# First layer: four conv chunks of w_in ahead of v, built up by quarters of the modulation

## The chip, the cores and the metric

The kernel runs on one core of one Trainium2 chip. The metric is the device time of one execution in microseconds (us). Engines are TensorE (PE, its weight loads PEld), VectorE (DVE), ScalarE (ACT), GpSimd (POOL) and SyncE (SP), which here issues nearly all DMA transfers.

## What is computed

A two-layer block over 512 tokens of x and 256 tokens of a context, 1024 features wide. For each layer:

```
mx, mc = split(silu(c) @ w_ada + b_ada, 6), the same of c_ctx      # the modulation
hx = rmsnorm(x, g) * (1 + mx[1]) + mx[0]; hc likewise with mc
z  = [hx; hc] @ w_in          # columns: q, k, v, o (512 each), 16 gates, fourier 256, conv a 256, conv t 256
u  = a * sigmoid(t);  yv = silu(layernorm(dwconv(u, 31 taps) + b_dw))
ym = mLSTM over q, k, v and the gates (4 heads, forward and backward), normed, times sigmoid(o)
yf = real part of a 2-D FFT of the fourier columns
x += mx[2] * rmsnorm(concat(ym, yf, yv) @ w_out);  x += mx[5] * rmsnorm(mlp(modulated norm of x))
```

The context takes the same steps in the first layer.

## The kernel before, in words

Tokens are in six blocks of 128: blocks 0 and 1 are the context, 2 to 5 are x. Features are in KB = 8 blocks of 128. The modulated, normalised input lies transposed in `hhi` and `hlo` (128 partitions, 8 feature blocks, 768 tokens): every fp32 operand is split into a high part and a rest, and each product is three matmuls, hi x hi, hi x lo, lo x hi. A weight is loaded by SP into one of three `raw` slots (L214), then ScalarE writes hi (L220) and VectorE writes lo = raw - hi (L221); there are six slots for hi and five for lo. `weight(...)` takes the next weight of the list `stream` and prepares up to `ahead` more.

Instructions are written in program order. A planner then orders each engine's instructions when the program is built: it prefers earlier ones but passes over what it reckons isn't ready. At run time each engine and each queue follows its order. `tc.cur_priority + LATER` (300) puts the conv taps behind 300 later instructions in that preference.

*Start of layer 0.* The modulation needed first (shift and scale of the mixers) comes in four quarters of its columns (`ada_first`). A quarter is 2 MB of w_ada, loaded by L299 into whatever slots are free (`rooms`: raw, hi, lo, t4 or halves of t3 tiles), multiplied with silu(c) (L313), given its bias (L316), turned into columns (L319, L320), scaled (L381) and applied by `prenorm_k` to two feature blocks of transposed x (transposes L446, then L453 on ScalarE, L233 and L234 on VectorE). The order of feature blocks is `KORD` = 0, 4, 1, 5, 2, 6, 3, 7, two per quarter. Between the quarters TensorE multiplies what is modulated with the first half of the v columns (`v_mm`, L511: 128 tokens stationary, 264 columns moving, 256 of v and 8 of gates), for the four x blocks in four `mm` PSUM banks. Then the context is loaded (L563), normalised (`unit`: L409, L398, L403, L411), modulated, and v is finished: 2 column halves x 6 blocks x 24 matmuls = 288. `v_out` evicts each (L516 on ScalarE, L517 on VectorE).

*After v.* The 16 gate columns in `gs` are transposed (L613) and pass through exp, ln and three-part scans on VectorE (L614 to L640), a round trip through DRAM (`md`, L638 to L653), and `gate_columns` (L659 to L671). Meanwhile `CHUNKS` runs: conv t0, a0, t1, a1, then q, k, o of four heads, then fourier. Each chunk is 128 columns of w_in by `stationary` (L464: 24 pairs of matmuls, 256 context tokens and 512 tokens of x, in two mm banks). t chunks end in a tanh (L967), a chunks in u = (tanh + 1) * a (L974). After a1 come `gate_columns` and the 62 taps of the depthwise convolution on VectorE (L688, L690), seven per chunk. Head h (`mlstm`) starts after chunk o of that head. After each chunk `background` runs three steps of the other modulations (a 512 KB load of w_a, L246, into a raw slot, and L248 on TensorE); they fill the same three raw slots as the weights.

Of the kernel before, what the change touches and what calls it, by code (L numbers as in the profile page):

```python
# [65 lines left out]
def build(tc, a):  # L66
# [216 lines left out]
    def ada_first(res):  # L283
# [4 lines left out]
        lo_ = lambda: lop.tile([128, 1024], F32, tag="lo", name=nm("raw"))  # L288
# [186 lines left out]
    def layer(l, res, nbg, first=None):  # L475
# [22 lines left out]
        vt = [t3()[:, :NB * 129].rearrange("p (b n) -> p b n", b=NB) for _ in range(H)]  # L498
        for h in range(H):
            P.memset(vt[h][:, :, 128:129], 1.0)  # L500
        gs = t3()[:, :NB * 128].rearrange("p (b n) -> p b n", b=NB)
        P.memset(gs, 0.0)
        gv = gs.rearrange("p b (g d n) -> p b g d n", g=2, d=2)
# [15 lines left out]
        if first is None:  # L519

# [24 lines left out]
        else:  # L545
            steps, xn = first[:2]
            xb = list(range(CB, NB))
            ps, ws = {}, ([], [])
# [6 lines left out]
            def some(c, bs, ms, p):  # L555
                for b in bs:
                    if (c, b) not in ps:
                        ps[c, b] = p()
                    v_mm(ps[c, b], b, ms, ws[c])

            ct = [t4() for _ in range(CB)]
            for b in range(CB):
                dma(ct[b], a["ctx"][128 * b:128 * b + 128, :])  # L563
# [3 lines left out]
            ws[0].append(weight("v", l, 0, 0, ahead=0))  # L567
            normed(0, pt)
            for q in range(4):
                if q == 3:  # L570
                    some(0, xb, [6, 7], mm)
                    break
                pt = [turned(xn, KORD[2 * q + 2 + m], 0) for m in range(2)]
                some(0, xb, [2 * q], mm)
                next(steps)
                if q < 2:
                    ws[0].append(weight("v", l, 0, q + 1, ahead=0))
                some(0, xb, [2 * q + 1], mm)
                next(steps)
                normed(q + 1, pt)  # L580
            ws[1][:] = [weight("v", l, 1, i, ahead=0) for i in range(2)]
            for b in xb:
                v_out(ps[0, b], 0, b)
            for b in range(CB):
                xn[b] = unit(ct[b])
# [3 lines left out]
            some(1, xb, range(2), mm)  # L589
            pt = [turned(xn, KORD[m], 1) for m in range(2)]  # L590
            for m in range(KB):
                if 2 <= m < VKB[1][1]:
                    some(1, xb, [m], mm)
                prenorm_k(pt.pop(0), KORD[m], res["Amix"], res["ac", 0], 0, 1)
                if m + 2 < KB:
                    pt.append(turned(xn, KORD[m + 2], 1))
            some(0, range(CB), range(KB), aux)
            for b in range(CB):
                v_out(ps[0, b], 0, b)
            ws[1].append(weight("v", l, 1, 2))  # L600
            some(1, xb, range(VKB[2][0], KB), mm)
            for b in xb:
                v_out(ps[1, b], 1, b)
            some(1, range(CB), range(KB), mm)
            for b in range(CB):
                v_out(ps[1, b], 1, b)
# [65 lines left out]

        y = {}


        u, cacc, tg = {}, {}, {}

        def conv_taps():
            for j in range(2):
                cacc[j] = t3()  # L680
            o0 = 0 if not last else XU
            o1 = UW - 2 * PAD
            for k in range(31):
                for j in range(2):
                    o = cacc[j][:, o0:o1]
                    w = hcol(C_DW, 2 * k + j)
                    if k == 0:
                        V.tensor_scalar(o, u[j][:, o0:o1], w, cols[:, C_BDW + j:C_BDW + j + 1], ALU.mult, ALU.add)  # L688
                    else:
                        V.scalar_tensor_tensor(o, u[j][:, o0 + k:o1 + k], w, o, ALU.mult, ALU.add)  # L690
                    yield

        def ccol(b):
            return 128 * b if b < CB else XU + 128 * (b - CB)

        def conv_norm():
            yt = [t3(), t3()]
            y[6], y[7] = yt
            for g in ([[2, 3, 4, 5]] if last else [[0, 1], [2, 3, 4, 5]]):
                xns, pss = [], []  # L700
                ba = tiny.tile([128, 4, 2], F32, tag="ba", name=nm("ba"))
                for i, b in enumerate(g):
                    if i % 2 == 0:
                        pss.append(aux())
                    for j in range(2):
                        c0 = 256 * (i % 2) + 128 * j
                        T.transpose(pss[-1][:, c0:c0 + 128], cacc[j][:, ccol(b):ccol(b) + 128], ident)
                for i in range(len(g)):
                    moments(pss[i // 2][:, 256 * (i % 2):256 * (i % 2) + 256], ba[:, i])
                r = rsd(ba, len(g))  # L710
                for i in range(len(g)):
                    if i % 2 == 0:
                        xns.append(c2())
                    cb = slice(256 * (i % 2), 256 * (i % 2) + 256)
                    V.tensor_scalar(xns[-1][:, cb], pss[i // 2][:, cb], ba[:, i, 0:1], r[:, i:i + 1],
                                    ALU.subtract, ALU.mult)
                yield
                back = [aux(), aux()]
                for i in range(len(g)):
                    for j in range(2):  # L720
                        c0 = 256 * (i % 2) + 128 * j
                        T.transpose(back[j][:, 128 * i:128 * i + 128], xns[i // 2][:, c0:c0 + 128], ident)
                n = 128 * len(g)
                t0 = 128 * g[0]
                for j in range(2):
                    z = yt[j][:, t0:t0 + n]
# [170 lines left out]
        def fourier(ws):  # L897
# [32 lines left out]
            for (t0, n) in segs:  # L930
                m = n // 2
                for pr in range(2):
# [6 lines left out]
                    V.tensor_tensor(yt[:, 1:m], yt[:, 1:m], ps[:, m + 1:n], ALU.add)  # L939


        taps = None
        got = {}
        staged = []

# [5 lines left out]
        for i, (n, j) in enumerate(CHUNKS):  # L951
# [16 lines left out]
            elif n == "a":  # L968
# [6 lines left out]
                if j == 1:  # L975
                    taps = conv_taps()
                    gate_columns()
# [499 lines left out]
```

## Time and profile before

| | us |
|---|---|
| three runs | 1513.02, 1516.81, 1517.34 (median 1516.81) |
| profiled execution, its own time | 1513.57 |
| its span, first to last instruction | 1511.9 |
| TensorE busy | 1471.7 (97%) |
| VectorE busy | 1093.8 (72%) |
| ScalarE busy | 757.9 (50%) |

The granted TensorE clock is 0.999 of full speed over the span. The time around the span is 1513.57 - 1511.9 = 1.67 us. Times in views count from the span's start.

### The profile page before, as it was taken

Reading aid. Unit: us, or ns where it says so; the run is one execution under the profiler, and the core shown is the slowest. Engines: PE = TensorE matmul, PEld = TensorE weight load, DVE = VectorE, ACT = ScalarE, POOL = GpSimd, SP = SyncE. Lnnn points to the kernel's source line nnn. Section 1 sums busy time; section 2 is a strip of 40 time slices with the busy share of each in tenths; the row PEclk is TensorE's granted clock in tenths of the full one; section 3 lists DMA queues with packets and bytes.
Section 4 is the critical chain, followed back from the end, with each engine's and each line's share of the span. In section 5 each row is a group of like instructions: output and inputs, shape, how many; then the busy total and the mean of one; then the engine's idle time right before and its main releaser. Section 6 shows DMA issues by size and latency. Waiting matters only on the chain. (4 is left out here: it accounts for less than half of the span.)

```text
span 1511.9 us, 23296 instructions
## 1 busy us (share of the span) xinstructions
PE 1471.7 (97%) x8894; PEld 1292.6 (85%) x8894; DVE 1093.8 (72%) x2155; ACT 757.9 (50%) x1523; POOL 84.4 (6%) x233
## 2 busy tenths in 40 slices
PE   7899999999999999999999999999999999999997
PEld 4878888987888898898988978888888889998887
DVE  3449987854899886766866576799666977667666
ACT  4632345535745352442524576544557555555544
POOL 0000012200000000000000010011111000000000
PEclk9999999999999999999999999999999999999999
DMA  8645436523532452432622252422225142333234
GB/s 317 156 140 206 158 122 219 207 70 123 183 126 96 144 193 72 166 136 88 195 76 92 80 183 97 133 84 76 107 84 180 43 126 98 112 112 100 83 95 143
DMA packets 68128, 197.32 MB, mean 131 GB/s; under 512 B 14064, under 2 KB 16528, under 8 KB 68016
## 3 DMA queue, kind: packets, MB, share of 16 engines
q1 hardware_dynamic: 66576, 191.11, 37.7%
q0 software_dynamic: 1440, 4.72, 1.0%
q8 instruction: 70, 1.15, 0.3%
q14 instruction: 42, 0.34, 0.1%
HBM read 183.14 MB, written 12.66 MB: 130 GB/s over the span
## 5 line engine op out<-in xcount | busy, mean ns | idle before, releaser
L220 ACT ACTIVATE hi<-raw 128x1024 fp32r<-128x1024 f32 (+1 forms) x245 | 244.0, 1000 | 375.8 <-PE mm L1074 141.6
L1074 PE MATMUL mm<-hi,t 128*128 128x512 f32 (+1 forms) x1296 | 406.4, 392 | 0.1
L221 DVE TENSOR_TENSOR lo<-raw,hi 128x1024 fp32r<-128x1024 f32 (+1 forms) x245 | 280.2, 1146 | 62.7 <-ACT hi L220 28.7
L1074 PEld LDWEIGHTS mm<-hi,t 128*128 128x128 f32 x1296 | 242.3, 188 | 54.9 <-DVE t L234 1.1
L1074 PE MATMUL mm<-lo,t 128*128 128x512 f32 (+1 forms) x648 | 253.4, 391 | 0.0
L464 PE MATMUL mm<-hhi,hi 128*128 128x256 f32 (+1 forms) x576 | 167.9, 336 | 0.0
L464 PE MATMUL mm<-hlo,hi 128*128 128x256 f32 (+1 forms) x576 | 165.8, 332 | 0.0
L464 PE MATMUL mm<-hhi,lo 128*128 128x256 f32 (+1 forms) x576 | 165.2, 331 | 0.0
L1074 PEld LDWEIGHTS mm<-lo,t 128*128 128x128 f32 x648 | 121.9, 188 | 26.3
L1143 PE MATMUL mm<-hhi,hi 128*128 128x384 f32 (+1 forms) x448 | 138.5, 309 | 1.8 <-ACT c L1169 1.7
L1143 PE MATMUL mm<-hhi,lo 128*128 128x384 f32 (+1 forms) x448 | 138.1, 308 | 1.5 <-DVE lo L221 1.5
L1242 DVE TENSOR_TENSOR t<-mm,t 128x512 f32<-128x512 f32 x120 | 81.6, 687 | 78.6 <-PE mm L1074 78.6
L1143 PE MATMUL mm<-hlo,hi 128*128 128x384 f32 (+1 forms) x448 | 138.0, 308 | 0.0
L464 PEld LDWEIGHTS mm<-hhi,hi 128*128 128x128 f32 x576 | 106.7, 188 | 14.9 <-issue 2.9
L464 PEld LDWEIGHTS mm<-hhi,lo 128*128 128x128 f32 x576 | 108.2, 188 | 10.8
L464 PEld LDWEIGHTS mm<-hlo,hi 128*128 128x128 f32 x576 | 107.8, 188 | 11.3 <-issue 0.8
L690 DVE SCALAR_TENSOR_TENSOR t<-t,half,t 128x783 f32<-128x783 f32 (+1 forms) x120 | 101.8, 886 | 0.4
L1143 PE MATMUL mm<-t,hi 128*128 128x384 f32 (+1 forms) x448 | 97.2, 308 | 0.0
L1143 PEld LDWEIGHTS mm<-hhi,hi 128*128 128x128 f32 x448 | 84.2, 188 | 3.9 <-ACT c L1169 2.2
L1143 PEld LDWEIGHTS mm<-hhi,lo 128*128 128x128 f32 x448 | 84.2, 188 | 1.9 <-DVE lo L221 1.9
L234 DVE TENSOR_TENSOR t<-c,t 128x256 fp32r<-128x256 f32 (+1 forms) x132 | 62.1, 477 | 32.5 <-ACT t L231 31.7
L1143 PEld LDWEIGHTS mm<-hlo,hi 128*128 128x128 f32 x448 | 84.2, 188 | 1.2
(254 smaller groups left out, 2706.1 us busy)
## 6 DMA issues: line engine op xcount, KB each, us to landing
raw<-w SPq DMA_DIRECT2D x128, 512.0 KB, 4.1
raw<-w_at SPq DMA_DIRECT2D x48, 512.0 KB, 3.5
raw<-w_a SPq DMA_DIRECT2D x44, 512.0 KB, 4.6
raw<-w_c SPq DMA_DIRECT2D x32, 512.0 KB, 4.2
xd<-t SPq DMA_DIRECT2D x20, 512.0 KB, 3.9
raw<-w_o SPq DMA_DIRECT2D x16, 512.0 KB, 5.3
t<-xd SPq DMA_DIRECT2D x20, 256.0 KB, 6.5
t<-x SPq DMA_DIRECT2D x8, 512.0 KB, 7.8
```

Source lines behind the costliest of these rows:

```text
L220: S.activation(hi[:, r0:n0], raw[:, r0:n0], AF.Copy)
L221: V.tensor_tensor(lo[:, r0:n0], raw[:, r0:n0], hi[:, r0:n0].bitcast(F32), ALU.subtract)
L234: V.tensor_tensor(blk_lo, src, blk_hi.bitcast(F32), ALU.subtract)
L464: T.matmul(o[:, :n], wp[:, k, :], hp[:, k, t0:t0 + n], start=k == 0 and i == 0, stop=k == KB - 1 and i == 2)
L690: V.scalar_tensor_tensor(o, u[j][:, o0 + k:o1 + k], w, o, ALU.mult, ALU.add)
L1074: T.matmul(ps, hp[:, 128 * b:128 * b + 128], wp[:, f % 2, c0:c1], start=f == fs[0] and at[0] == 0 and n == 0, stop=f == fs[-1] and at[1] = ...
L1143: T.matmul(ps[:, :HN], wp[:, K2 * j + k, :], hp, start=first and k == 0 and i == 0, stop=k == K2 - 1 and i == 2, skip_group_check=True)
L1242: V.tensor_tensor(ac_, ps, ac_, ALU.add)
```

## The change

In layer 0 the four conv chunks come first, and v after them. The weights' list is reordered to match. `ada_first` loads the chunks' weights in place of the first half of w_v: two chunks behind quarter 0, two behind quarter 1, and the context behind quarter 2; the quarters lie in other slots (quarter 0 in four hi slots, quarter 1 in eight halves of t3, quarter 2 in two hi slots and four halves, quarter 3 in eight halves). Transfers of w_ada by halves of t3 are 256 KB, the others 512 KB.

The chunks are built up in the quarters for the 512 tokens of x, in four mm banks: quarter 0 with chunks 0 and 1, quarter 1 with chunks 2 and 3 too. The context is normalised after quarter 0 and modulated quarter by quarter. Its 256 tokens are multiplied apart from x: chunks 0 and 1 in two aux banks, chunks 2 and 3 in mm banks when x is done. Then v runs densely over six blocks and two halves; after each block two conv taps are written, after each third block a `background`. Then come the gates as before, q0, k0, with `gate_columns` after k0 (in layer 1 it stays after a1), o0 and the rest, with seven taps per chunk until the 62 are done.

```diff
     for l in range(DEPTH):
+        if l == 0:
+            for i, (n, j) in enumerate(CHUNKS[:4]):
+                stream.append(((n, l, j), a["w_c"][l, i], (KB, 128)))
...
         for i, (n, j) in enumerate(CHUNKS):
+            if l == 0 and i < 4:
+                continue
...
-        rooms = ((raw_, raw_, raw_, t4), (hi_, hi_, hi_, lo_), (lo_, raw_, raw_, raw_), (half_,) * 6 + (raw_,))
+        rooms = ((hi_,) * 4, (half_,) * 8, (hi_,) * 2 + (half_,) * 4, (half_,) * 8)
...
-            if q < 3:
-                pre["v", 0, 0, q] = t3()[:, :264 * (VKB[q][1] - VKB[q][0])]
-                dma(pre["v", 0, 0, q].rearrange("p (k n) -> p k n", n=264), a["w_v"][0, 0, :, VKB[q][0]:VKB[q][1], :])
+            if q < 2:
+                for i in (2 * q, 2 * q + 1):
+                    key = (CHUNKS[i][0], 0, CHUNKS[i][1])
+                    pre[key] = raw_()
+                    dma(pre[key].rearrange("p (k n) -> p k n", k=KB), a["w_c"][0, i])
+            elif q == 2:
+                res["ct"] = [t4() for _ in range(CB)]
+                for b in range(CB):
+                    dma(res["ct"][b], a["ctx"][128 * b:128 * b + 128, :])
...
+        def tap(n):
+            for _ in range(n):
+                if conv["taps"] is None:
+                    return
+                prio = tc.cur_priority
+                tc.cur_priority = prio + LATER
+                done = next(conv["taps"], 1) == 1
+                tc.cur_priority = prio + 1
+                if done:
+                    staged.append(conv_norm())
+                    conv["taps"] = None
...
+            def normed_ctx(q):
+                for k in KORD[2 * q:2 * q + 2]:
+                    prenorm_k(turned(xn, k, 1), k, res["Amix"], res["ac", 0], 0, 1)
+            def take(i):
+                cw.append(weight(CHUNKS[i][0], l, CHUNKS[i][1], ahead=0))
+            def some(items, v, p):
+                t0, n = CX[v]
+                for j, m in items:
+                    if (j, v) not in ps:
+                        ps[j, v] = p()
+                    (hi, lo), k = cw[j], KORD[m]
+                    for i, (wp, hp) in enumerate(((hi, hhi), (hi, hlo), (lo, hhi))):
+                        T.matmul(ps[j, v][:, :n], wp[:, k, :], hp[:, k, t0:t0 + n],
+                                 start=m == 0 and i == 0, stop=m == KB - 1 and i == 2)
+            def done(v):
+                for j in range(4):
+                    conv_in(*CHUNKS[j], ps[j, v], *CX[v])
+            next(steps)
+            pt = [turned(xn, KORD[m], 0) for m in range(2)]
+            next(steps)
+            take(0)
+            take(1)
+            normed(0, pt)
+            for b in range(CB):
+                xn[b] = unit(res["ct"][b])
+            plan = (([(0, 0), (1, 0)], [(0, 1), (1, 1)]),
+                    ([(j, m) for j in (2, 3) for m in (0, 1)], [(j, m) for m in (2, 3) for j in range(4)]),
+                    ([(j, 4) for j in range(4)], [(j, 5) for j in range(4)]))
+            for q in range(3):
+                pt = [turned(xn, KORD[2 * q + 2 + m], 0) for m in range(2)]
+                if q == 1:
+                    take(2)
+                    take(3)
+                some(plan[q][0], 1, mm)
+                next(steps)
+                some(plan[q][1], 1, mm)
+                next(steps)
+                normed(q + 1, pt)
+                normed_ctx(q)
+            some([(j, m) for j in range(2) for m in range(6)], 0, aux)
+            some([(j, m) for m in (6, 7) for j in range(4)], 1, mm)
+            normed_ctx(3)
+            done(1)
+            some([(j, m) for j in range(2) for m in (6, 7)], 0, aux)
+            some([(j, m) for j in (2, 3) for m in range(KB)], 0, mm)
+            done(0)
...
+            vt, gs, gv = v_tiles()
+            conv["taps"] = conv_taps()
+            for c in range(2):
+                ws = [weight("v", l, c, i) for i in range(len(VKB))]
+                for b in range(NB):
+                    ps_ = mm()
+                    v_mm(ps_, b, range(KB), ws)
+                    v_out(ps_, c, b)
+                    tap(2)
+                    if b % 3 == 2:
+                        background()
...
         for i, (n, j) in enumerate(CHUNKS):
+            if first is not None and i < 4:
+                continue
...
             elif n == "k":
                 got["k"] = short_conv(outs, lambda k: dk[:, k, j:j + 1], ranges)
+                if first is not None and j == 0:
+                    gate_columns()
```

`conv_in` holds the tanh and the product that the chunk loop held (L967 to L974), for one range of tokens; `v_tiles` allocates what stood ahead of v (L497 to L503).

## Rows read from the trace of the kernel before

**Rows 1.** Page, part 1: busy us (share of the span) and instructions.

```profile
PE 1471.7 (97%) x8894; PEld 1292.6 (85%) x8894; DVE 1093.8 (72%) x2155; ACT 757.9 (50%) x1523; POOL 84.4 (6%) x233
```

**Rows 2.** Stretches: length, PE, PEld, DVE, ACT, POOL busy (instructions), clock, DMA share, GB/s.

```profile
26.00:48.70 22.70, 20.07 (x271) 16.95 (x271) 9.94 (x26) 6.50 (x11) 0.00 (x0) 1.00 0.83 238
48.70:60.00 11.30, 9.70 (x76) 9.24 (x77) 4.64 (x11) 9.87 (x26) 1.43 (x8) 1.00 0.65 132
60.00:79.20 19.20, 19.20 (x158) 19.20 (x157) 7.83 (x19) 10.07 (x27) 0.00 (x0) 1.00 0.35 111
79.20:95.00 15.80, 15.80 (x109) 13.02 (x109) 9.57 (x10) 8.83 (x13) 0.00 (x0) 1.00 0.29 102
95.00:111.00 16.00, 13.92 (x93) 10.63 (x91) 7.07 (x9) 1.27 (x2) 0.00 (x0) 1.00 0.70 211
111.00:160.00 49.00, 49.00 (x339) 39.82 (x339) 45.97 (x64) 14.60 (x31) 2.91 (x20) 1.00 0.52 184
```

**Rows 3.** Waits of TensorE, 22.5 to 60 us: us in total, times, longest.

```profile
PE mm L511 <- DVE hhi L233: 1.8, 1, 1.8
PE mm L511 <- DVE t L517: 0.9, 1, 0.9
PE aux L313 <- ACT c L453: 0.8, 2, 0.4
PE aux L446 <- ACT t L411: 0.7, 1, 0.7
```

**Rows 4.** Waits of TensorE, 60 to 111 us.

```profile
PE aux L248 <- DMA raw<-w_a: 2.1, 2, 1.4
```

**Rows 5.** Waits of TensorE, 111 to 320 us.

```profile
PE aux L785 <- DVE c L889: 3.2, 3, 1.2
```

**Rows 6.** Stretches again, PE and PEld of L511 alone, then of L464 alone.

```profile
60.00:79.20 19.20, 19.20 (x152) 18.70 (x150) 1.00 0.35 111
...
80.30:88.40 8.10, 8.04 (x46) 7.02 (x46) 1.00 0.14 55
```

**Rows 7.** Timeline of ScalarE, 19 to 62 us: start, us, instruction, [idle before].

```profile
24.96 1.61 ACT L220 ACTIVATE hi<-t 128x792 fp32r<-128x792 f32 x2
...
32.47 1.44 ACT L453 ACTIVATE c<-aux,ac,A 128x512 f32<-128x512 f32 x2 [5.89 <-PE aux L446]
```

**Rows 8.** Timeline of VectorE, 0 to 125 us.

```profile
26.57 0.98 DVE L221 TENSOR_TENSOR lo<-t,hi 128x792 fp32r<-128x792 f32 x1
...
82.30 0.95 DVE L618 SCALAR_TENSOR_TENSOR t<-t 64x768 f32<-64x768 f32 x1 [2.20 <-ACT t L615]
...
95.89 0.95 DVE L640 TENSOR_TENSOR t<-t,t 64x768 f32<-64x768 f32 x1
96.87 1.23 DVE L221 TENSOR_TENSOR lo<-raw,hi 128x1024 fp32r<-128x1024 f32 x1
```

**Rows 9.** Transfers from 0 to 44 us, GB/s in 40 slices of 1.1 us.

```profile
GB/s 0 68 113 359 380 305 197 357 405 386 402 417 417 402 409 395 414 417 417 409 400 413 417 413 417 385 385 394 404 378 102 19 15 4 156 417 406 416 408 355
```

**Rows 10.** Timeline of SP's DMA queue, 10 to 62 us: start, us of issuing.

```profile
23.08 6.56 SPq L299 DMA_DIRECT2D t<-w_a  x6
36.41 0.33 SPq L299 DMA_DIRECT2D raw<-w_a  x1
...
46.22 7.08 SPq L354 DMA_DIRECT2D bac<-bcol  x2
53.40 0.95 SPq L214 DMA_DIRECT2D raw<-w_c  x2
```

**Rows 11.** Stretches, L690 (conv taps) alone: length, DVE busy (instructions), clock, DMA.

```profile
111.00:165.00 54.00, 33.48 (x34) 1.00 0.49 170
```

**Rows 12.** Waits of SP's queue, 0 to 125 us: us in total, times, longest.

```profile
SPq L246 <- DVE lo L221: 8.0, 3, 6.2
...
SPq L299 <- DMA raw<-w_a: 7.0, 8, 1.1
SPq L299 <- PE aux L313: 6.9, 3, 5.9
```

More of the change, by code (lines that the diff above doesn't have):

```diff
@@ L495, in layer, with conv_in @@
             yield "norm", res["Amix"]
[L498 to L503, printed above, removed]
+        y, u, cacc, tg = {}, {}, {}, {}
+        staged = []
+        conv = {"taps": None}
+        def conv_in(n, j, o, t0, m):
+            if n == "t":
+                if j not in tg:
+                    tg[j] = t3()
+                S.activation(tg[j][:, t0:t0 + m], o[:, :m], AF.Tanh, scale=0.5)
+                return
+            if j not in u:
+                u[j] = t3()
+                for z0 in (0, PAD + CTX, UW - PAD):
+                    P.memset(u[j][:, z0:z0 + PAD], 0.0)
+            d0 = PAD if t0 == 0 else 2 * PAD + CTX
+            V.scalar_tensor_tensor(u[j][:, d0:d0 + m], tg[j][:, t0:t0 + m], 1.0, o[:, :m], ALU.add, ALU.mult)
@@ new lines, in tap, with conv_taps @@
+        def tap(n):
+            for _ in range(n):
+                if conv["taps"] is None:
+                    return
+                prio = tc.cur_priority
[5 more added lines that the diff above has]
+                    conv["taps"] = None
+        def conv_taps():
+            for j in range(2):
+                cacc[j] = t3()
+            o0 = 0 if not last else XU
+            o1 = UW - 2 * PAD
+            for k in range(31):
+                for j in range(2):
+                    o = cacc[j][:, o0:o1]
+                    w = hcol(C_DW, 2 * k + j)
+                    if k == 0:
+                        V.tensor_scalar(o, u[j][:, o0:o1], w, cols[:, C_BDW + j:C_BDW + j + 1], ALU.mult, ALU.add)
+                    else:
+                        V.scalar_tensor_tensor(o, u[j][:, o0 + k:o1 + k], w, o, ALU.mult, ALU.add)
+                    yield
@@ L588, in layer @@
             dma(bd, a["bd"])
[L589 to L606, printed above, removed]
+            vt, gs, gv = v_tiles()
+            conv["taps"] = conv_taps()
[8 more added lines that the diff above has]
+                        background()
         li, x = t3()[0:64, :TOK], t3()[0:64, :TOK]
@@ L671, in gate_columns @@
             S.activation(dec, dec, AF.Exp)
[L673 to L726, printed above, removed]
-                    th = c2()
-                    S.activation(z, back[j][:, :n], AF.Identity, scale=hcol(C_GLN, j), bias=hcol(C_BLN, j))
-                    S.activation(th[:, :n], back[j][:, :n], AF.Tanh, scale=hcol(C_GLN, j), bias=hcol(C_BLN, j))
-                    V.scalar_tensor_tensor(z, th[:, :n], 1.0, z, ALU.add, ALU.mult)
-                yield
@@ L986, in layer @@
                 staged.append(mlstm(j, got["q"], got["k"], to))
-            if taps is not None:
-                for _ in range(TAPS):
-                    prio = tc.cur_priority
-                    tc.cur_priority = prio + LATER
-                    done = next(taps, 1) == 1
-                    tc.cur_priority = prio + 1
-                    if done:
-                        staged.append(conv_norm())
-                        taps = None
-                        break
+            tap(TAPS)
             background()
-        if taps is not None:
-            for _ in taps:
+        if conv["taps"] is not None:
+            for _ in conv["taps"]:
                 pass
```

89 lines of the change are left out of this document (50 added, 39 removed).

## Prediction

> **What bounds the kernel now.** I read the engine shares first: TensorE is busy for 97% of the span [rows 1], so a reordering without new arithmetic can win only what TensorE stands still, and lose only where it makes it stand. The table of stretches then says where that is [rows 2]. From 26.0 to 48.7 us, where the four quarters of the first modulation arrive, TensorE is busy 20.07 of 22.70 us (2.63 lost); from 48.7 to 60.0 it is busy 9.70 of 11.30 (1.60 lost); then it is full until 95.0, loses 2.08 us until 111.0, and is full again until 160. The waits name the losses. Between 22.5 and 60 us [rows 3]: 1.8 us for hhi of the last quarter (nothing is left to multiply until it is modulated), 0.9 us for a PSUM bank that v's eviction L517 frees, 0.8 us where the next quarter's L313 waits until L453 frees an aux bank, 0.7 us for the normalised context (L411). Between 60 and 111 us all 2.1 us are L248 waiting for its w_a block [rows 4]. After 111 us, 3.2 us are head outputs, three times, for VectorE [rows 5]. So about 4.2 + 2.1 + 3.4 = 9.7 us can be had at the very most; what it idles before 22.5 us belongs to x and quarter 0, whose transfers stay in front.
>
> VectorE matters for the second half of the change: it is busy 7.83 of 19.2, 9.57 of 15.8 and 7.07 of 16.0 us in the stretches from 60 to 111 us, then 45.97 of 49.0 [rows 2].
>
> **The change, part by part.** *Matmuls.* Layer 0 keeps its 288 matmuls of v and the 192 of the four conv chunks. In the dense v stretch 152 L511 run in 19.20 us, 0.126 us each at most; 46 L464, pairs of 256 and 512 columns, take 8.10 us, 0.352 a pair [rows 6]. Now the 512s and the 256s run apart. The 264-column v matmuls show that narrow ones keep their pace alone; 256/264 of 0.126 is 0.122, which leaves 0.230 for a 512. I take 0; the bounds are plus or minus 96 x 0.004 = 0.4 us.
>
> *The quarters.* Before, a quarter feeds TensorE 24 matmuls of v, 24 x 0.126 = 3.0 us. After, quarter 0 gives 12 x 0.230 = 2.8 us, quarter 1 gives 36 x 0.230 = 8.3, quarter 2 gives 24 x 0.230 = 5.5, and 36 context matmuls, 36 x 0.122 = 4.4 us, stand ready before quarter 3 is needed. These 4.4 us cover the 1.8 us wait; it goes, and comes back whole if the context is late. The 0.9 us bank wait goes too: the mm banks are now freed by conv_in while 12 context matmuls (1.5 us) run; without that cover it stays 0.9. The 0.7 us goes, because the context is normalised from quarter 0 on. The 0.8 us I keep: two context transposes more per quarter use the same four aux banks; bounds 0 and 2.4 (all three quarters waiting as long as both waits of the row together). Gain 1.8 + 0.9 + 0.7 = 3.4 us.
>
> *Splits.* The first weights are 1024 columns, not 792. Before, ScalarE makes the two hi parts from 24.96 in 1.61 us [rows 7] and VectorE the first lo by 26.57 + 0.98 = 27.55 [rows 8]. Scaled by columns, c0's hi comes 0.2 us later and c1's lo, the last that quarter 0 needs, at about 29. The eight hi-only matmuls (1.8 us) and quarter 1's L313 lie in front of it. I charge 0.5 us, bounds 0 and 1.5.
>
> *Transfers.* SP's order changes. Ahead of quarter 2 come 4 x 512 KB of w_c in place of 396 + 396 KB of w_v: 1.26 MB more, 3.1 us at 410 GB/s [rows 9]. Summing the slices of that row, quarter 2's last byte (9.8 MB) is in by about 28 us; 31 us is still ahead of its use, which follows the L453 of 32.47 [rows 7], at about 33.3. Ahead of quarter 3's end come 2.0 MB more (w_c and context, less w_v), 5.0 us. But in the kernel before its last block waits at 36.41, because its raw slot is held until quarter 2's L313 has read it (a wait of 5.9 us [rows 12]): transfers pause about 5 us (the slices of 102 to 156) [rows 9, 10]. Quarter 3 now lies in t3 tiles, so the pause goes and the bytes take its place: 0, hidden by quarter 1's 8.3 us of matmuls. The change moves 20 blocks of 256 KB where there were 6. The six of before went out at 23.08 to 29.64 [rows 10], and the slices there hold 378 to 417 GB/s [rows 9], so I charge nothing. The Trainium skill (DMA: Bandwidth & Descriptors, Measured) speaks against this: it wants transfers of 1 MiB or more, and lists 341 GB/s at 1 MB and 138 at 64 KB; by the 341 the 9.4 MB of w_c, context and three quarters would take, as an estimate, 4.7 us longer than at 410; the slices of the trace differ from it.
>
> The new wait is the fourth w_c block. There are three raw slots, so it can leave only when c0's lo is written, about 26.57 + 1.23 = 27.8 us [rows 8]. Its turn in SP's order comes earlier: L299 waits eight times for a transfer before it [rows 12], so some eight blocks are under way, and the turn is there when about 6.4 MB have landed, 20 us [rows 9]. Behind it: quarter 2, context, quarter 3. I take 0, since the order on SP is not the program's: layer 1's bias (L354) leaves at 46.22, ahead of the w_c blocks of 53.40 [rows 10], so what isn't ready is passed. The other bound is a rival.
>
> *Conv taps.* 34 of them take 33.48 us after 111 us [rows 11]; 24, some 24 us, are now put into v's 288 x 0.126 = 36 us, where VectorE otherwise has v's small copies and six splits of about 1 us: hidden. If they delay a copy that frees a bank, three other mm banks of 3.0 us each cover it. VectorE is freed of them later. Of the 3.2 us of L785 waits I take 0.6, half of the longest; bounds 0 and 3.2.
>
> *Gates and background.* L613 to L640 move from beside the conv chunks to beside q0 and k0. Before, the scans hold VectorE until 95.89 + 0.95, and the split of a w_c block starts right behind at 96.87 [rows 8]; SP's w_a loads wait 8.0 us in all for such splits [rows 12], and that is how L248 comes to stand 2.1 us. During v there are no scans, only taps: I take back 1.0, and leave the rest, because the scans now meet the splits of k0 and o0. Bounds 2.1 back, or 2.1 more.
>
> Sum: -3.4 + 0.5 - 0.6 - 1.0 = -4.5 us. The profiled execution took 1513.57 us (span 1511.9), so 1509.1; the median of the runs is 1516.81, and in proportion 1512.3.
>
> **Rivals.** *More goes.* If all rows of waits from 26 us on fall, 9.7 us: 1507. For it: TensorE's slack may be larger than its idle time. Its weight loads are busy 16.95 of 22.70 us in the quarters, 75%, against 18.70 of 19.20, 97%, in the dense stretch [rows 2, 6]; against it, many loads there belong to short 32-column L313. The Trainium skill (Perfetto Trace Analysis, Identifying the Most-Contended Engine) says that matmul busy time is a poor measure of headroom and weight-load share a good one; by it, at 97%, the quarters lose 22.70 - 16.95/0.97 = 5.2 us instead of 2.63.
>
> *The waits only move.* Context transposes and four splits crowd the aux banks and ScalarE; each quarter's chain gets as much longer as its cover. 3.4 us stay, the time is 1516. For it: TensorE's order is fixed, and a wait at its head holds all behind it.
>
> *SP stands at the fourth block: slower.* If that load is ordered ahead of quarter 2, nothing leaves from 20 to 27.8 us. What is under way (8.5 MB in all) has landed by 25; quarter 2 then ends at 27.8 + 1.5 + 2.6/0.41 = 35.7 us (1.5 from the load of 36.41, whose bytes show in the slices from 37.4 on), 2.4 late against its use at 33.3. The context is in at 38.3, with L409 and L411 behind it (1.1 to 1.2 us each, twice), so that its transposes can hold TensorE up to 7 us more: -4.5 + 9.4 = +4.9, 1521.7. It decides when fewer than three of quarter 2's loads pass the fourth block.
>
> *Gates late.* The chain from L618 (82.30) to L640's end (96.84) is 14.5 us [rows 8], plus the md round trip, where VectorE is 94% busy [rows 2]. Before, most of three conv chunks, 24 x 0.352 = 8.4 us each, lie between it and L659; after, q0 and k0 alone, 16.9 us, and L659 stands in TensorE's order behind them. Taken as 3 us of waiting there, and at L248 2.1 more in place of 1.0 less: 1518.
>
> *Half-size blocks slow the transfers*, the rule above: at the 378 of the lowest full slice in place of 410 [rows 9], 9.4 MB take 2.0 us longer, mostly covered: 1513. I give it 0.03 inside the second rival.
>
> **Numbers.** Forecast 0.44 (its own range 1509 to 1516), more goes 0.18, waits only move 0.18, SP stands 0.12, gates late 0.08. What a measurement of this kernel can tell from no change is about 0.3%, 4.5 us. The forecast lies on that edge, so half of it counts as faster: 0.22 + 0.18 = 0.40. Same: the other 0.22, 0.14 of the moved waits, 0.04 of the gates = 0.40. Slower: 0.12 + 0.04 + 0.04 = 0.20. The range, from the larger gain to the standing queue, is 1506 to 1521.
>
> **What would show it.** Right: no wait for hhi of the last quarter; no wait of L299 for L313 on SP; the last quarter's L453 later than 47 us without TensorE idling; first taps before 90 us; fewer than 2 us lost between 26 and 60. Wrong: TensorE waiting at a context transpose or at L313 for w_a; an SP wait of several us before quarter 2's loads; a wait at L659; VectorE's splits late during q0 and k0. The prediction fails most easily through the order that the planner gives TensorE, which the trace of before can't show.

## The result, and the profile after

The changed kernel takes 1525.67 us (median of 4, 1523.45 to 1527.33) where the kernel before, timed beside it, takes 1515.65 (1513.02 to 1517.34): a ratio of 1.0067, 95% interval 1.0045 to 1.0088. It is slower, and the time lies above the predicted range. The profiled execution has a span of 1523.0 us, 11.1 more than before. The page's first part answers to [rows 1]: hardly any work was added.

```profile
PE 1476.5 (97%) x8894; PEld 1293.9 (85%) x8894; DVE 1095.5 (72%) x2155; ACT 758.6 (50%) x1523; POOL 86.6 (6%) x233
```

The same stretches as in [rows 2], and two short ones within them:

```profile
22.50:26.00 3.50, 2.84 (x72) 2.08 (x69) 2.43 (x7) 1.45 (x2) 0.00 (x0) 1.00 1.05 410
26.00:48.70 22.70, 18.41 (x136) 14.21 (x129) 8.43 (x15) 12.05 (x18) 2.26 (x13) 0.85 0.79 243
48.70:60.00 11.30, 9.25 (x100) 7.13 (x100) 4.76 (x13) 4.81 (x8) 0.53 (x8) 1.00 0.65 133
60.00:79.20 19.20, 18.27 (x124) 16.27 (x123) 8.79 (x19) 7.85 (x16) 0.00 (x0) 1.00 0.20 60
79.20:95.00 15.80, 15.80 (x141) 14.90 (x140) 15.76 (x22) 2.65 (x9) 0.00 (x0) 1.00 0.51 186
95.00:111.00 16.00, 15.91 (x141) 14.57 (x143) 14.61 (x20) 4.45 (x12) 0.00 (x0) 1.00 0.49 163
111.00:160.00 49.00, 45.27 (x326) 36.19 (x319) 46.13 (x66) 19.02 (x41) 1.81 (x1) 0.97 0.53 166
...
28.70:35.10 6.40, 5.77 (x13) 4.35 (x14) 5.12 (x7) 3.89 (x5) 0.00 (x0) 0.50 0.58 194
147.90:151.40 3.50, 3.50 (x16) 2.13 (x15) 3.50 (x8) 1.37 (x4) 0.00 (x0) 0.53 0.45 71
```

The column to look at is the clock, which was 1.00 in every row of [rows 2]. From 28.7 to 35.1 us it is 0.50, the lower of the two levels (1.2 of 2.4 GHz). There 13 products take 5.80 us (29.33 to 35.13), and 13 of the same take 3.05 us from 37.03 on: 2.75 us lost while TensorE counts as busy. At 147.9 to 151.4 us it is 0.53, which costs 1.6 us more (0.47 of 3.5).

Length minus PE busy, against before, gives the rest: 0.6 us more idle at 22.5 to 26, 1.7 at 26 to 48.7, 0.5 to 60, 0.9 to 79.2, 3.7 at 111 to 160, 2.5 at 205 to 280 and 0.9 at 320 to 360; against these, 2.0 less at 95 to 111, and 2.2 less in three other stretches (before 22.5, 160 to 205, 280 to 320). That is 6.7 us of standing still and 4.4 us of half clock, 11.0 of the 11.1. After 360 us the two kernels work at the same pace.

The waits of TensorE at 22.5 to 60, 60 to 111 and 111 to 320 us answer to [rows 3, 4, 5] ("issue" is a wait for nothing that the profile shows):

```profile
PE mm L666 <- ACT hi L225: 2.3, 1, 2.3
PE aux L323 <- issue: 1.5, 1, 1.5
PE aux L323 <- ACT c L463: 0.9, 2, 0.5
PE aux L456 <- ACT t L421: 0.5, 1, 0.5
...
PE aux L666 <- ACT c L463: 0.9, 1, 0.9
...
PE aux L850 <- DVE t L863: 2.7, 1, 2.7
PE aux L768 <- DVE t L749: 2.7, 1, 2.7
PE aux L834 <- DVE c L938: 1.3, 1, 1.3
PE aux L253 <- DMA raw<-w_a: 1.0, 2, 0.7
```

Nearly all that was to go did go: the 1.8 us for hhi of the last quarter, the 0.9 us for v's bank, the 2.1 us for w_a at 95 to 111; the 0.7 us for the normalised context is 0.5. Four new places, (A) to (D), cost more. Two of them show in the timelines of TensorE, then of ScalarE (the groups x1 of products between are left out):

```profile
26.70 0.36 PE L329 MATMUL aux<-sel_sb,c 128*128 128x8 f32 x2 [0.51 <-DVE c L326]
29.33 0.79 PE L666 MATMUL mm<-hhi,hi 128*128 128x512 f32 x1 [2.27 <-ACT hi L225]
...
45.08 0.44 PE L456 MATMUL aux<-ident_sb,t 128*128 128x128 f32 x2 [0.47 <-ACT t L421]
46.06 1.08 PE L323 MATMUL aux<-raw,csil 128*32 128x128 f32 x32 [0.55 <-ACT c L463]
```

```profile
27.55 0.78 ACT L463 ACTIVATE c<-aux,ac,A 128x512 f32<-128x512 f32 x1 [3.27 <-DVE A L391]
28.23 1.99 ACT L225 ACTIVATE hi<-raw 128x1024 fp32r<-128x1024 f32 x2
...
38.43 1.06 ACT L419 ACTIVATE t<-t 128x1024 f32<-128x1024 f32 x1 [3.03 <-DMA t<-ctx]
```

(A) ScalarE stands still from 24.3 to 27.55 us with the first convolution weight's hi part to make, because a modulation of quarter 1 is ahead of it in its order. (B) Quarter 2's modulation products (L323) start at 46.06, behind all 48 products that quarters 0 and 1 allow and behind the context's transposes, which wait for L421. (C) On VectorE the gates' chain took 14.5 us before, with nothing between its steps. Now L727 starts it and L749 ends it at 147.21, after 21.1 us. Among its scans stand three taps (L549), a weight's split (L226) and two steps of the short convolution of q and k (L799), 6.4 us together:

```profile
126.11 0.95 DVE L727 SCALAR_TENSOR_TENSOR t<-t 64x768 f32<-64x768 f32 x1 [0.41 <-ACT t L724]
126.98 3.85 DVE L549 SCALAR_TENSOR_TENSOR t<-t,half,t 128x783 f32<-128x783 f32 x4
...
131.63 1.02 DVE L549 SCALAR_TENSOR_TENSOR t<-t,half,t 128x783 f32<-128x783 f32 x1
...
142.85 1.02 DVE L799 SCALAR_TENSOR_TENSOR t<-t,cols,t 128x769 f32<-128x769 f32 x1
...
146.26 0.95 DVE L749 TENSOR_TENSOR t<-t,t 64x768 f32<-64x768 f32 x1
```

(D) The third head's masked scores (L850) wait for md's load. On SP's queue it leaves behind two loads of w_o; ScalarE stands 4.31 us for it (SP's queue first, then ScalarE):

```profile
254.15 1.46 SPq L219 DMA_DIRECT2D raw<-w_o  x2
256.08 0.57 SPq L272 DMA_DIRECT2D gd<-c  x2
256.70 0.39 SPq L873 DMA_DIRECT2D c<-md  x1
```

```profile
263.35 1.49 ACT L860 ACTIVATE t<-c,pcol 128x256 f32<-128x256 f32 x4 [4.31 <-DMA c<-md]
```

Also SP did stand at the fourth w_c block, 6.2 us, and let it go at 30.68; four of quarter 2's six loads had left before it. The experiments tell which of these cost what.

### The profile page after: what moved, and what is told of

It reads as the page before. It is cut to its first block, busy times and chain, and to the rows that moved or that the text cites. A ratio compares the mean times of both kernels' runs of the same rounds, so it can differ in the third digit from the quotient of the medians.

```text
span 1523.0 us, 23311 instructions
## 1 busy us (share of the span) xinstructions
PE 1476.5 (97%) x8894; PEld 1293.9 (85%) x8894; DVE 1095.5 (72%) x2155; ACT 758.6 (50%) x1523; POOL 86.6 (6%) x233
## 5 line engine op out<-in xcount | busy, mean ns | idle before, releaser
L226 DVE TENSOR_TENSOR lo<-raw,hi 128x1024 fp32r<-128x1024 f32 (+1 forms) x248 | 282.8, 1143 | 69.6 <-ACT hi L225 35.0
L474 PE MATMUL mm<-hhi,hi 128*128 128x256 f32 (+1 forms) x512 | 151.6, 336 | 0.0
L474 PE MATMUL mm<-hhi,lo 128*128 128x256 f32 (+1 forms) x512 | 149.3, 332 | 0.0
L474 PE MATMUL mm<-hlo,hi 128*128 128x256 f32 (+1 forms) x512 | 149.2, 332 | 0.0
L474 PEld LDWEIGHTS mm<-hhi,hi 128*128 128x128 f32 x512 | 95.4, 189 | 12.5 <-issue 3.3
L474 PEld LDWEIGHTS mm<-hhi,lo 128*128 128x128 f32 x512 | 96.4, 189 | 9.4
L474 PEld LDWEIGHTS mm<-hlo,hi 128*128 128x128 f32 x512 | 96.4, 189 | 9.4
L549 DVE SCALAR_TENSOR_TENSOR t<-t,half,t 128x783 f32<-128x783 f32 (+1 forms) x120 | 101.7, 887 | 0.3
L1177 PEld LDWEIGHTS mm<-hhi,hi 128*128 128x128 f32 x448 | 84.3, 188 | 4.3 <-ACT c L1203 2.0
L1177 PEld LDWEIGHTS mm<-hhi,lo 128*128 128x128 f32 x448 | 84.4, 188 | 1.9 <-DVE lo L226 1.9
L1177 PEld LDWEIGHTS mm<-hlo,hi 128*128 128x128 f32 x448 | 84.4, 188 | 1.2
```

The costliest lines, as they stand in the source:

```text
L226: V.tensor_tensor(lo[:, r0:n0], raw[:, r0:n0], hi[:, r0:n0].bitcast(F32), ALU.subtract)
L474: T.matmul(o[:, :n], wp[:, k, :], hp[:, k, t0:t0 + n], start=k == 0 and i == 0, stop=k == KB - 1 and i == 2)
L1177: T.matmul(ps[:, :HN], wp[:, K2 * j + k, :], hp, start=first and k == 0 and i == 0, stop=k == K2 - 1 and i == 2, skip_group_check=True)
```

## Experiments

Each kernel was timed beside the kernel before, whose own median was 1514.3 to 1515.7 us from sitting to sitting; so rows of different sittings compare best by their ratios, and a microsecond between two medians says little. Gains below are between medians unless a ratio is named. Line numbers move a little with an edit; the tiles tell which operation it is. The quarters are numbered 0 to 3; "third" is quarter 2. The turn is L329, which turns a quarter's modulation into columns.

| kernel | median us | ratio to before, 95% |
|---|---|---|
| changed kernel | 1525.67 | 1.0067 (1.0045 to 1.0088) |
| 1 hi first | 1524.19 | 1.0062 (1.0047 to 1.0077) |
| 2 gates later | 1522.80 | 1.0050 (1.0034 to 1.0067) |
| 3 fourth slot | 1523.95 | 1.0064 (1.0042 to 1.0087) |
| 4 = 1+2+3 | 1520.96 | 1.0043 (1.0028 to 1.0058) |
| 5 = 4 + quarter 2 ahead | 1523.85 | 1.0069 (1.0053 to 1.0084) |
| 6 = 5 + context behind | 1518.66 | 1.0034 (1.0020 to 1.0047) |
| 7 changed, no background in v | 1530.32 | 1.0109 (1.0088 to 1.0130) |
| 8 changed, no taps in v | 1530.62 | 1.0113 (1.0084 to 1.0142) |
| 9 = 6 + w_v's splits later | 1513.16 | 0.9986 (0.9974 to 0.9998) |
| 10 = 9 + md on GpSimd's queue | 1518.20 | 1.0022 (1.0010 to 1.0034) |
| 11 = 10 + turn earlier | 1514.28 | 0.9998 (0.9983 to 1.0014) |
| 12 = 9 + turn earlier | 1511.09 | 0.9968 (0.9957 to 0.9978) |
| 13 = 12 + md in t3, all heads | 1515.22 | 0.9990 (0.9979 to 1.0001) |
| 14 = 12 + md in t3, third head | 1512.35 | 0.9976 (0.9964 to 0.9988) |

**1 to 4: the four places, each alone, then three together.** 1 puts quarter 1's modulation behind the two hi parts on ScalarE, 2 moves the first layer's gate columns behind o's first chunk, 3 gives the fourth w_c block a slot of its own (comments added).

```diff
+            hi1 = st["hi"]                       # 1: last hi part of chunk 1
...
+                    with tc.issue_after(hi1):
+                        normed(q + 1, pt)
...
-                if first is not None and j == 0: # 2: at "k"; now at "o"
-                    gate_columns()
...
-                    pre[key] = raw_()            # 3
+                    pre[key] = raw_() if i < 3 else lop.tile([128, 1024], F32, tag="lo", name=nm("raw"))
```

> The changed kernel with one thing different: ScalarE must write the hi parts of the first two conv weights before it modulates quarter 1. Theory (TensorE stands at c0's hi from 27 to 29.3 us, the granted clock then falls to half for 6.5 us): the 2.3 us wait goes, the clock stays at 1.00 from 26 to 49 us, in all about 5 us less than the changed kernel, ratio to before near 1.004. Rival (the late quarter 2 and context behind the fourth w_c block are the loss, the hi wait only sits in front of it): the first matmuls come earlier but TensorE waits as much longer at 44 to 50 us, less than 2 us gained, ratio 1.006.

> The changed kernel with gate_columns of layer 0 written after the first o chunk in place of the first k chunk. Theory (L768's transposes stand at the head of TensorE's order for the scans, 2.7 us, with 0.75 us at L253 before them and half clock for 3.4 us behind): all of it goes, 3.5 us of waiting and 1.6 of clock, ratio near 1.003. Rival (VectorE is the bound of that stage, so the wait moves to the scores of head 0 or to a weight's lo): under 2 us, ratio 1.006.

> The changed kernel with the fourth w_c block in a slot of the lo pool, so that SP needn't wait for c0's lo (it stood from 24.1 to 30.7 us). Theory of the order (quarter 2's L323 stands behind 46 conv matmuls and two context transposes in TensorE's order, so its landing doesn't matter): transfers of quarter 2 and context land some 3 us earlier, the time changes by under 1 us, ratio 1.006. Rival (SP's stand is the loss): 3 to 5 us gained, ratio 1.004.

> All three together: hi parts first, gate_columns after the first o chunk, the fourth block in a lo slot. Theory: the sum, 5 + 5 + 0.5 us, leaves about 1515, ratio 1.000, with quarter 2's chain (some 3 us lost between 44 and 50 us in the changed kernel) as the loss that stays and the w_a waits as the gain. Rival: each stand is replaced by the next, ratio above 1.004.

Each took away the wait that it was aimed at; what each alone gave in time is not settled, since the three intervals overlap that of the changed kernel. 1: the first product at 27.4 us, clock 1.00 at 28 to 35; but TensorE then ran out of products sooner (43.71: 1.93 us at a context transpose), and the clock was 0.5 at 45.8 to 52.7 instead, so the time stayed, as the rival expected (the cause that it named, the fourth block, is what 3 tests). 2: 111 to 160 us went from 3.73 to 1.02 us idle at clock 1.00; its median is 2.9 us lower, between its theory and its rival. 3: SP no longer stands at that block, and the medians differ by 1.7 us, so the standing queue alone was not the cause. Together their median is 4.7 us lower (3.6 by the ratios), where the theory had 10.5: the rival. What was left stands in the TensorE timeline of 4:

```profile
38.81 1.31 PE L456 MATMUL aux<-ident_sb,t 128*128 128x128 f32 x10 [1.37 <-ACT t L421]
...
43.04 1.08 PE L323 MATMUL aux<-raw,csil 128*32 128x128 f32 x32 [0.32 <-ACT c L463]
...
47.90 0.36 PE L329 MATMUL aux<-sel_sb,c 128*128 128x8 f32 x2 [2.91 <-DVE c L326]
```

Quarter 2 comes when the 48 products that quarters 0 and 1 allow are used up; nothing covers its chain, and the clock falls again (0.51 at 48.3 to 51.4). Of the 2.91 us, 2.5 lie in a bias add that started late (see the last section).

**5 and 6: quarter 2's order, and the context's.** 5 puts the last 12 of those products behind quarter 2's 64 L323. 6 normalizes the context behind quarter 2's modulation, and transposes it after quarter 3's.

```diff
+                    with tc.issue_after(res["am"]):     # 5: res["am"] = last L323
+                        some(plan[q][1], 1, mm)
...
-                normed_ctx(q)                           # 6
+                if q == 1:
+                    with tc.issue_after(st["mod"]):
+                        for b in range(CB):
+                            xn[b] = unit(res["ct"][b])
+                elif q == 2:
+                    for c in range(3):
+                        normed_ctx(c)
```

> Built on the kernel with all three edits (1520.96 us). The third quarter's 64 modulation products (L323) are put ahead of the last 12 of the 48 convolution products that the first two quarters allow; before, they stood behind all 48. Theory (TensorE's order around this quarter is what is left): the chain from its products over the bias add, the turn and the modulation on ScalarE to the split is then covered by those 12 (2.8 us) and 8 transposes (2 us); the 2.9 us wait for the bias add and the stretch at half clock at 48.3 to 51.4 us (1.6 us lost) go: 1516 to 1517.5. Rival (the context): four transposes of the context still stand ahead of the L323, and the context is normalized only at about 42 us, so TensorE waits there and the L323 start no sooner than 42 us: 1520 to 1522, with the waits on L421 kept.

> As the run before it, and the context's two blocks are normalized on ScalarE behind the modulation of the third quarter, their transposes after the fourth quarter. Theory of the order: no further gain over the run before (1516 to 1518), or a loss, since the context's modulation comes on top of ScalarE later. Theory of the context: this is the edit that frees TensorE at 37 to 48 us; the L323 of the third quarter end by 38 us, the waits on L421 (1.9 us) and on the bias add (2.9 us) go with the stretch at half clock (1.6 us): 1514.5 to 1516.5, and the clock is 1.00 in every stretch.

The rival of 5 held, and it was worse than that: L323 starts at 42.54, still behind L456 for L421 (0.93 and 1.93 us). A wait of 3.8 us at a transpose is new: it needs an aux bank that quarter 2's modulation (L463) frees, and in this kernel's order ScalarE has a split of w_v ahead of that modulation and stands 8.5 us for the load:

```profile
52.06 0.86 ACT L225 ACTIVATE hi<-raw 128x792 fp32r<-128x792 f32 x1 [8.50 <-DMA raw<-w_v]
52.83 2.35 ACT L463 ACTIVATE c<-aux,ac,A 128x512 f32<-128x512 f32 x4
```

6 did what 5 could not: all but two of quarter 2's 64 L323 run from 37.18 us on, 5.4 us sooner than in 5. One line of its TensorE timeline, and its stretches:

```profile
37.18 0.96 PE L323 MATMUL aux<-raw,csil 128*32 128x128 f32 x27
```

```profile
26.00:48.70 22.70, 21.76 (x224) 16.88 (x216) 9.95 (x20) 7.24 (x12) 2.08 (x14) 1.00 0.84 253
48.70:60.00 11.30, 8.28 (x38) 6.00 (x33) 5.34 (x15) 8.89 (x16) 0.37 (x9) 0.85 0.39 120
```

0.94 us idle at 26 to 48.7 us, where the kernel before has 2.63 and 4 has 6.05: the context was what stood ahead. The 5.2 us that 6 is below 5 are not all the context's, since 5's split of w_v no longer stands ahead of quarter 2 either. Against 4 the medians differ by 2.3 us and the ratios by 0.0009, within their intervals. The time is 2 to 4 us above what was expected, because quarter 3 now waits at 52 to 57 us. Its ScalarE stood 3.83 us at a split for w_v's load, ahead of L421 and L463, and VectorE 2.21 us at the second layer's L494 for the load of cols.

**7 and 8: parts undone.** 7 leaves out the four `background()` calls in the loop over v, 8 the `tap(2)` there.

> The changed kernel without the four calls of background() in the loop over v. Theory: those four steps move the later loads of w_a, and with them the load of md for the masked heads falls back on SP's queue; without them the waits of 2.7 and 0.94 us at 262 and 326 us go, and the load's wait at 144 us (0.75): 1521 to 1523. Rival: the steps are taken at the chunks anyway, and the order of the taps sets it: 1525 to 1526, with the wait at 262 us kept.

> The changed kernel without the taps between the blocks of v (they start at the first chunk behind it, as in the kernel before they started behind the fourth chunk). Theory: the scans of the gates are then not interleaved with taps on VectorE, the gate chain takes its 14.5 us again, the wait on t L749 (2.7 us) goes and so does the stretch at half clock at 148 to 151 us (1.6 us); the taps end later: 1521 to 1523. Rival: VectorE, which then does nothing during v, is late afterwards with taps and splits, and what is gained at 147 us is lost at 160 to 280 us: 1525 to 1529.

Both lost 5 us. In 7 the wait (D) fell from 2.7 to 1.2 us, but the waits at the gate columns (L766, 2.7 us in the changed kernel) and for head outputs (L832, 1.3 there) grew to 3.7 and 2.8 us: the theory's waits shrank and its time did not come. In 8 VectorE is busy 5.62 of 31 us at 80 to 111 and 70.12 of 75 at 205 to 280; TensorE then waits for the taps and the convolution's norm behind them, 5.8 us idle at 280 to 320 alone. So the taps in v are a gain, as counted. The wait at the gate columns is 1.1 us there, 2.7 with the taps: they are a part of (C). For the background steps only the time says so: of the 2.4 us that 7's profiled execution is longer than the changed kernel's, about 1.9 lie at 22.5 to 60, ahead of the edit (clock 0.86 there, 0.91 in the changed kernel).

**9 to 12: quarter 3, md's queue, the turn.** 9 puts w_v's first splits behind the context's last modulation on ScalarE, and the second layer's dk and half behind its last split on VectorE. 10 issues md's loads on GpSimd's queue. 11 and 12 put the turn (L329) of quarters 2 and 3 behind 6 products, not 12.

```diff
+            if key[:3] == ("v", 0, 0):                  # 9
+                with tc.issue_after(st["mod"]):
+                    S.activation(hi[:, r0:n0], raw[:, r0:n0], AF.Copy)
...
+            with tc.issue_after(st["mlo"]):             # 9: dk, half
+                halves()
...
+                (dma if first is None else P.dma_start)(mb, ...)   # 10
...
+                        some(plan[q][1][:2], 1, mm)     # 11, 12
+                    next(steps)
+                    with tc.issue_after(res["tm"]):
+                        some(plan[q][1][2:], 1, mm)
```

> On the kernel with the context behind the third quarter (1518.66 us): ScalarE splits w_v's first blocks only behind the last modulation of the context, and VectorE computes the second layer's dk and half (which wait for a load of cols) behind the context's last split. In the kernel that this is built on, the context's second pass (L421) and the fourth quarter's modulation stood behind a split that waited 3.8 us for w_v, and VectorE's L494 waited 2.2 us for cols ahead of that quarter's split. Theory (fixed orders hold the fourth quarter too): at 48.7 to 60 us 2 of the 3.0 us of idle TensorE go, and the clock is 1.00 there (1.7 us more): 1514 to 1516. Rival (the fourth quarter's chain has no cover in any order, since only 24 products of it and no context stand ready): 1517.5 to 1519, idle and half clock kept at 52 to 58 us.

> As the run before it, and in the first layer the loads of md for the heads are issued on GpSimd's queue in place of SP's, so that they no longer stand behind w_o's loads, which wait for VectorE's splits. Theory: the wait on the masked scores at 255 to 259 us (3.1 us) goes, and the clock of 205 to 280 us is 1.00 again (3 us at most): 3 to 5 us below the run before it. Rival: the load comes no sooner, because its buffer is held by the convolution's norm (PE L581) until the same time, or GpSimd's queue waits at the loads of dft ahead of it: no change within 1 us.

> As the run before it, and in the third and fourth quarters the turn of the modulation (L329) stands behind 6 of the 12 convolution products ahead of it, not behind 12, so that the chain from there to the split starts 1.4 us sooner and 6 products are left to cover it. Theory: what is left of TensorE's wait for hhi at 52 to 57 us becomes smaller by 1 to 1.4 us: 1 us below the run before it, at most 2.5 with the clock. Rival: the chain was covered already, or the products are missed before the turn as much as they help behind it: no change.

> The kernel with w_v's splits later (1513.16 us) and the turn behind 6 of 12 products, with md's loads back on SP's queue. In the two runs before it, the turn had brought 3.9 us beside the loads on GpSimd's queue, whose own loss was 5.0 us. Theory (the two add up): 26 to 60 us has under 1 us of idle TensorE at clock 1.00; 1509 to 1512, faster than the kernel before by 0.2 to 0.4%. Rival (part of the 3.9 us was the clock in 205 to 280 us, which falls in one execution and not in another): 1512 to 1514.

9 gained 5.5 us and is just below the kernel before. At 48.7 to 60 us its profile shows what was expected, 0.65 us idle at clock 1.00 where 6 has 3.02 at 0.85. A part of the gain was not aimed at: at 250 to 265 us the clock is 1.00 behind a wait of 2.7 us, where 6 has 0.77 behind 3.1: an estimated 3.5 us (0.23 of 15). 10 lost 5.0: its load left no earlier than in 9 (245.33 us, 244.47 in 9), behind two loads of dft on GpSimd's queue, and ScalarE got it at 255.49, 10.2 us later, against 6.6 in 9 (251.06); the scores waited 5.3. The load came no sooner, as the rival had it, and the time is worse than the rival's; why the load took longer no run shows. The Trainium skill (Trainium Kernel Development and Optimization, Key Constraints) says that issuing transfers from several engines saves only the sequencer's time; the trace agrees that nothing was to be had there. The turn gave 3.9 us beside 10 and 2.1 beside 9, where I had 1 to 2.5; beside 10, 2.8 us of idle time went at 22.5 to 60 (3.34 to 0.52), and the clock at 205 to 280 rose from 0.95 to 0.98. The stretches of 12, which beats the kernel before by 0.3% (0.2 to 0.4) and the changed one by 1%:

```profile
26.00:48.70 22.70, 21.89 (x214) 16.94 (x211) 10.24 (x21) 9.64 (x15) 2.69 (x21) 1.00 0.73 248
48.70:60.00 11.30, 11.30 (x74) 9.78 (x73) 4.75 (x13) 6.02 (x14) 0.00 (x0) 1.00 0.56 157
```

0.81 us idle in place of the 4.23 of [rows 2] and the 6.34 of the changed kernel, at full clock.

**13 and 14: md's buffer.** `mb = t3()[:, :512]` in place of one of the five c2 tiles: for all heads, then for the third alone.

> As the run before it, and the context's part of md for a head is loaded into a tile of the large pool (t3) in place of one of the five c2 tiles, which the convolution's norm holds; its load then stands ahead of the last two of w_o on SP's queue. Theory (the buffer holds the load, and so the masked scores): the wait of 2.7 us on the scores at 248 to 260 us goes: 2 to 3 us below the run before it. Rival (the scores wait for the exponentials' chain ScalarE, GpSimd, VectorE in any case, or the large pool is short): no change within 1 us, or a new wait on a t3 tile.

> As the run of 1511.09 us, and only the third head's part of md for the context goes into a tile of t3. In the run before, where all four heads had it so, the third head's load landed 7 us earlier and the wait of 2.6 us at 250 to 258 us was gone, but the first head's load had fallen behind loads of w_a on SP's queue (issued at 150.74 in place of 141.81 us), the scores waited 3.1 us at 155 to 158 us, and the clock was 0.96 and 0.84 in the stretches from 140 to 165 us. Theory (the c2 buffer holds the third head's load; the first head's new wait was the whole price): the order up to 235 us is that of 1511.09, the third head's wait goes and no new one comes: 1508 to 1509.5. Rival (the large pool or VectorE sets the scores in any case): 1510.5 to 1512.

In 13 the third head's load leaves at 238.01 us (243.37 in 12), and its wait is gone. But the first head's fell behind loads of w_a; SP's queue and TensorE's timeline of 13:

```profile
142.33 8.32 SPq L255 DMA_DIRECT2D raw<-w_a  x3
150.74 0.39 SPq L901 DMA_DIRECT2D t<-md  x1
```

```profile
158.50 2.93 PE L878 MATMUL aux<-t,t 128*128 128x256 f32 x12 [3.13 <-ACT t L915]
```

In 14 that is mended, and the third head's wait (2.6 us in 12) is gone too, but the time is that of 12 within the intervals: the waits of 205 to 360 us of 14 are now others, 4.7 us where 12 has 4.2.

```profile
PE aux L862 <- DVE c L966: 3.2, 2, 2.3
PE aux L918 <- ACT c L600: 1.5, 1, 1.5
```

So the buffer and the queue held the load (shown), and the load was not what bounds that stretch: the rival. What does, among VectorE's chains there, stays open.

## Why the prediction was wrong

Idle time against before and the loss by the clock, added up stage by stage, set beside the forecast's terms:

| stage | forecast, us | measured, us |
|---|---|---|
| 22.5 to 60, without the wait for the first hi part | -3.4 | +0.5 |
| the wait for the first hi part and the half clock behind it | +0.5 | +5.0 (2.3 + 2.75) |
| 95 to 111 and 111 to 160 (gates and background) | -1.0 | +3.4 (-2.0, +3.7, +1.6 by the clock) |
| 160 to 360 (taps) | -0.6 | +1.6 |
| before 22.5, and 60 to 79.2 | 0 | +0.6 |
| sum | -4.5 | +11.1 |

*Matmuls (0).* Right: 13 products of 512 columns take 3.05 us at full clock, 0.235 each, where 0.230 was taken.

*The quarters (-3.4 us).* Here the forecast failed: the cover was counted in amounts and not in order. Of the 3.4 us of waits, 2.9 did go, and the "36 context matmuls" that were to "stand ready before quarter 3 is needed" did cover it: they run from 62.49, after 0.9 us for an aux bank, with no wait for hhi. But in TensorE's fixed order the context's transposes, which they need, stood ahead of quarter 2's L323 and waited for ScalarE, so that these start at 46.06 where the forecast had them at about 33.3; and new waits of about the same sum came at transposes, turns and L323 (1.5 us of it, at 56.89, without a releaser in the profile). So the rival "the waits only move" describes this stretch. Run 6 shows the step: with the context behind quarter 2, its L323 run from 37.18 us in place of 43.04 (run 4), and 26 to 48.7 us has 0.94 us idle in place of 6.05. In time it gave little (2.3 us against run 4) until quarter 3's order was mended too: run 12 has 0.81 us idle at 26 to 60, 3.4 less than before, the size of the term.

*Splits (+0.5, bounds 0 to 1.5).* The other failed step. I scaled the hi part's duration and took its start from before; its start was set by the modulation ahead of it on ScalarE. It cost 2.3 us of waiting, beyond the bound, and the half clock behind it. Run 1 removes both there; the time then went to the next place, quarter 2.

*Transfers (0).* Right as far as the runs tell: SP stood at the fourth block (6.2 us), but four of quarter 2's loads had passed, where its rival asked for fewer than three, and without the stand run 3 is 1.7 us faster where that rival asked for 9.4. Small blocks: 410 GB/s at 22.5 to 26 us, no loss.

*Conv taps (-0.6).* The first tap is at 79.1 us, as said, and the wait for head outputs fell from 3.2 to 1.3 us up to 320 us, more than I took; 0.9 more stand at 320 to 360, where there was none. Not counted was that the taps meet the gates' scans (C), nor the new wait (D): from 160 to 360 us the changed kernel loses 1.6 us.

*Gates (-1.0).* The 2.1 us at 95 to 111 us went whole. But the rival "gates late" came true with its 3 us: 2.7 at L768, and 1.6 by the clock, which it did not have. The forecast let the scans meet the splits of k0 and o0 within 2.1 us; taps and the short convolution stood between them as well. Run 2 removes the wait.

*The clock* was in no term, since it was 1.00 in every row. It made 4.4 of the 11 us. In the changed kernel two waits of 2 to 3 us cost 2.75 and 1.6 us more by the clock (2.27 us at the first hi part, 2.70 at L768); a third, 2.73 us at L850, cost nothing more.

*The rivals.* The moved waits and the late gates came together, and SP stood besides, at no clear price; I had priced them as if one excluded the others. Three of the four signs of being wrong that the prediction names came: a wait at a context transpose, SP's stand (ahead of two of quarter 2's loads), the wait at the gate columns. The hardest to see was (D): nothing in the change touches the third head, but SP's order does. Runs 9 and 12 show that the mechanism itself pays: with the orders set by hand the same reordering is 0.3% faster than before. That its -4.6 us (against its own 1515.66) is close to the -4.5 of the forecast is partly luck: by the profiles 26 to 60 and 95 to 111 us win 3.4 and 2.1 us, and 111 to 160 and 205 to 280 lose 2.5 and 3.1 idle.

## What to carry to other kernels

Cover is a matter of order: when work is moved to hide a wait, write down for each engine what stands ahead of the first instruction of the hidden chain, the loads of later stages included, and pin that order where a planner might choose another. A wait on TensorE of 2 to 3 us should be priced at between once and about twice its length, since in these runs the clock fell behind some such waits and not behind others. Mend orders in sequence and look again after each: here mends 1, 5 and 6 each moved a loss to the next place.

## What the runs showed of the hardware

I had not expected the granted clock to answer to such short waits. After 2.27 us of standing still (27.06 to 29.33, with two 8-column products before it) the row says 0.50 for 28.7 to 35.1 us; after 2.70 us at 144.66 to 147.36 it says 0.53 for 3.5 us. Yet after 2.7 us at L850 in the changed kernel the stretch 205 to 280 shows 1.00, and run 10 shows 0.95 there after 5.3 us. The Trainium skill (TensorE: Matmul & The Clock Gate, HAM oscillation) describes a kernel whose waits for loads bring the clock down each time; the trace agrees for some waits here, and not for others. What sets them apart stays open. Also unexplained: in run 4 VectorE's bias add L326 started 2.5 us after the last L323 that it needs had ended (45.0 to 47.47), for a releaser that the profile calls remote; in run 2 it was 1.7 us (49.6 to 51.28), and in the changed kernel and run 6 the same took 0.1 us.
